# Keys and values of latents and context computed as an eighth seven-product group, with keys stored by tokens

## The chip, the cores and the metric

The kernel runs on one core of a Trainium2 chip. The metric is device time in microseconds of one execution; the kernel before takes 1354.65 us (median of three runs: 1354.47, 1354.65 and 1359.87 us). The engines are PE (TensorE matmuls), DVE (VectorE), ACT (ScalarE), POOL (GpSimd) and SP (SyncE); transfers are issued from SP, ACT and POOL, each of which has a queue of its own and works through it in program order.

## The reference, cut to what matters

One layer of a diffusion block works on 512 latent tokens `x` and 256 context tokens `ctx`, with D = 2048.

```python
shift, scale, gate = split(silu(c) @ w_ada + b_ada)          # also with c_ctx, for the context
h  = rmsnorm(x,   norm_g) * (1 + scale)   + shift            # 512 x 2048
hc = rmsnorm(ctx, norm_g) * (1 + scale_c) + shift_c          # 256 x 2048
kc, vc = hc @ w_in[:, K], hc @ w_in[:, V]                    # 4 heads of 128 each; kc is head-normed
p  = h @ w_in                                                # q, k, v, z_a, u_b, z_b, g_a, g_b
q, k = rope(rmsnorm(q)) * 128**-0.5, rope(rmsnorm(k))
attn = softmax(q @ concat(k, kc).T) @ concat(v, vc)          # 12 query heads, 4 key heads, 768 keys
y = (sigmoid(g_a) * ((attn * silu(z_a)) @ w_pa)
   + sigmoid(g_b) * ((fft2_real(u_b) * silu(z_b)) @ w_pb)) @ w_out
out = rmsnorm(x + gate * y, final_g)
```

Everything is in float32. The kernel splits each operand into a high and a low float32r part and forms a product from three matmuls (high by high, high by low, low by high).

## The kernel before, in words

**Start** (the modulation, the loop at L564). For each of the 16 blocks `kb` of 128 features, 2 MB of `w_ada` come in by two transfers (L392, from POOL for all but the first two blocks, four buffers in turn), 32 small matmuls (L476) and two turns (L486) give shift and scale, and `make_h` (L464 to L466) writes the high and low part of h for that block. Between these, `start_work` multiplies with the columns of u_b and z_b (8 tiles of 128) and of V for the latents (4 tiles): 16 blocks x 12 tiles x 3 = 576 matmuls of 128x512, whose weights come by SP (L177) and are split by ACT (L141) and DVE (L142). Partial sums are kept in SBUF by L506 and L508 after each group of blocks.

**Forms.** `form_row(j)` (L548 to L560) runs after the loop in program order, for j = 0 to 7. It adds up high and low of blocks j and j + 8 on DVE, forms S3, Z5, S2 and S4 for the seven-product scheme in one buffer `f` (one for all eight rows, L550), and stores it to `f_d` from POOL (L560). Row j + 1 writes the buffer that the store of row j reads.

**Fourier stage** (L594 to L671). `halves` (L605, L606) adds and subtracts halves of u_b, then come splits, `channels` (matmuls with `fch`), `positions` (matmuls with `fsq`), and a product with silu(z_b) (L643). Its memory lies over the buffers of the start, so its first instruction waits until those are free.

**Keys and values** (L674 to L768). Plain products: K of the latents and of the context, and V of the context, for six token tiles of K and two of V, 8 x 16 x 3 = 384 matmuls of 128x512; the context is loaded (L650 and in `context_rows`), normed and modulated here. Keys are head-normed, rotated, turned by PE (L734) and stored turned (L737).

**Seven groups by seven products** (`Group`, L821). Each takes 1024 columns of w_in (three groups of q and z_a, four of the gates g_a and g_b) and forms the 512 x 2048 by 2048 x 1024 product as two by two blocks with seven block products instead of eight. A product has four pieces of weights; a piece is 12 matmuls; a group is 7 x 4 x 12 = 336. Weights are combined in four SBUF tiles `R`, partly by transfers that add (L226, from POOL), partly by DVE (L215, L217), and split ahead of their use (L141, L142) by as many pieces as there are split buffers (3, then 5 from group 0's second product on). `job()` (L808, called at L851) runs one waiting side task after each piece.

**Attention, branches and output** (L1028 on). `get_keys` takes K and V of a group of three heads, 48 steps compute scores, softmax and values, then come the output projections, the gated merge and two more seven-product groups.

The engines run in the order that the build gives each of them; the build moves instructions ahead of others where its own model lets it. A transfer queue is served in that order too.

Of the kernel before, what the change touches and what calls it, by code (L numbers as in the profile page):

```python
# [58 lines left out]
NQZ, NGATE = 3, 4  # L59
# [7 lines left out]
def between(g, name, pc):  # L67

    f = {"P1": "Z5", "P2": "S2", "Q6": "S3", "P7": "S4"}.get(name)
    return [(f, pc - 1)] if f and g == 0 and pc in (1, 2) else []  # L70
# [4 lines left out]
def start_pieces():  # L75
# [18 lines left out]
def block_kernel(ctx, tc, xT, ctxT, x, c_row, w_ss, w_gate, vecs, qkg, rope, dft_c, dft_s,  # L94
                 w_start, w_kv, w_g, w_pab, w_o, final_g, out):
# [10 lines left out]
    bst, bpool = region("bpool", "right")  # L106
    rc = bpool.tile([P, C], F32, name="rc")
    dsc = ctx.enter_context(tc.tile_pool(name="dsc", bufs=1, space=DRAM))
    gs = dsc.tile([KK, P], F32, name="gs")
    k_d = dsc.tile([NKV, P, NKEY], F32, name="k_d")  # L110
# [26 lines left out]
    def bank2():  # L137
        return ps.tile([P, 1024], F32, tag="b2", bufs=2, name=uid("pd"))
# [58 lines left out]

    def hl_tiles():
# [4 lines left out]
        if isinstance(pool, int):  # L203
            return [Halves([pairs[2 * pool + k][i][:, :, 256:] for k in range(2)]) for i in range(2)]
# [102 lines left out]
    s_tiles = []  # L307

# [33 lines left out]
    def stream_keys(g):  # L342
        stream(("K", g), k_d[g], NKEY, 1, dst=lambda: tiles(g))
        stream(("V", g), flat(v_d[g]), NKEY, KT, dst=lambda: tiles(g))


    DONE = {"P2": (0, 0), "P7": (1, 1), "Q3": (0, 1), "Q4": (1, 0)}
    for g in range(NQZ + NGATE):
        for name in ONE_GROUP:
            if (g, name) == (NQZ + NGATE - 1, "Q4"):  # L350
                stream_keys(0)
            stream_product(name, g, w_g[g], BY_DVE_GATES)
# [28 lines left out]
    bbst, bbpool = region("bb", "right")  # L381
    bb = bbpool.tile([P, 4, T], F32, name="bb")
    pst, ppool = region("part", "right")
    part = ppool.tile([P, NS, T], F32, name="part")
    vals = ppool.tile([P, 4, T], F32, name="vals")
# [24 lines left out]
    def squares(srcs, n, r, new, run):  # L410

        acc = bank2()
        for q in range(0, KK, 2):
            a, b = new(), new()
            for t, src in zip((a, b), srcs(q)):
                nc.scalar.activation(t, src, ACT.Square)
            nc.vector.tensor_tensor(a, a, b, op=ALU.add)
            if q == 0:
                nc.vector.tensor_copy(run, a)
            else:  # L420
                nc.vector.tensor_tensor(run, run, a, op=ALU.add)
        nc.tensor.matmul(acc[:, :n], ones, run, start=True, stop=True)
        nc.scalar.activation(r, acc[:, :n], ACT.Sqrt, bias=eps_t[:, 0:1], scale=1.0 / D)
        nc.vector.reciprocal(r, r)

    def token_norms():
# [6 lines left out]
        acc = bank2()[:, :T]  # L433
# [17 lines left out]
    def spread(pick, r):  # L451
        acc = bank()
# [27 lines left out]
    def columns(acc, kb):  # L480
# [3 lines left out]
        sp = acc[:, 512:768]  # L484
# [15 lines left out]
    def start_work():  # L500
        ends = {kb + nk for kb, nk in GROUPS}
        begins = {kb for kb, nk in GROUPS}

# [6 lines left out]
        vacc = None  # L510
        for p in start_pieces():
            kb, nk, t, nt = p[2:]
            wh, wl = get(("start", p))
            if t >= 0:
                for i in range(nt):
                    acc = bank()
                    c = slice(P * i, P * i + P)
                    for k in range(nk):
                        mm3(acc, wh[:, k, c], wl[:, k, c], hhi[kb + k], hlo[kb + k], k == 0, k == nk - 1)
                    keep(pt(t + i), acc, kb == 0)  # L520
                    yield 3 * nk
            else:
                if kb in begins:
                    vacc = [bank() for _ in range(4)]
                for i in range(4):
                    c = slice(P * i, P * i + P)
                    for k in range(nk):
                        mm3(vacc[i], hhi[kb + k][:, c], hlo[kb + k][:, c], wh[:, k, :], wl[:, k, :],
                            kb in begins and k == 0, kb + nk in ends and k == nk - 1)
                    if kb + nk in ends:  # L530
                        keep(vals[:, i, :], vacc[i], kb == 0)
                    yield 3 * nk
# [9 lines left out]
    wacc = bank()  # L542
# [21 lines left out]
    for kb in range(KK):  # L564
# [22 lines left out]
    pa.close()  # L587
    for _ in work:
        pass
    for t in range(4):  # L590
        nc.gpsimd.dma_start(v_d[:, :, t, :].rearrange("g p d -> p g d"), vals[:, t, :].rearrange("p (g d) -> p g d", g=4))

    hX, lX = (lambda k: hhi[k]), (lambda k: hlo[k])

# [36 lines left out]
    def positions(g):  # L631
# [11 lines left out]
        nc.vector.scalar_tensor_tensor(alt(bb[:, g, :]), acc.rearrange("p (e s) -> p e s", e=2), 1.0 / 256.0,  # L643
                                       alt(part[:, 4 + g, :]), op0=ALU.mult, op1=ALU.mult)

    crs, crp = region("cr", "right")

    def ct_load(q):
        ct = crp.tile([P, 2, C], F32, tag="ct", bufs=2, name=uid("ct"))
        nc.sync.dma_start(ct, ctxT[:, q : q + 2, :])  # L650
        return ct[:, 0, :], ct[:, 1, :]
# [860 lines left out]
```

## Time and profile before

| | |
|---|---|
| median of three runs | 1354.65 us |
| the profiled execution | 1359.74 us, its span 1358.0 us |
| granted TensorE clock, mean | 0.994 |
| PE busy | 1319.7 us (97% of the span) |
| DVE busy | 983.8 us (72%) |
| ACT busy | 672.8 us (50%) |
| POOL busy | 145.6 us (11%) |
| moved by DMA | 294.16 MB, 217 GB/s on the mean |

A row of the timeline gives start, duration, engine, line, operation, output and input, shape and count, and in brackets the idle time before it and what ended it. A row of windows gives for each engine the busy time and the number of instructions in a stretch, then the granted clock, the share of the DMA engines' time and GB/s. Matmuls overlap in the records (a 128x512 one is recorded with about 390 ns), so their cost is read from the distance between starts.

### The profile page before, as it was taken

The numbers are of one execution on the slowest core, as the hardware profiler recorded it, in microseconds if no ns is written. First come the engines' busy times: TensorE is split into PE (matmuls) and PEld (weight loads), VectorE is DVE, ScalarE is ACT, GpSimd is POOL, SyncE is SP. The second block draws the span as 40 slices with busy tenths as digits, with TensorE's granted clock in tenths as the row PEclk, the third lists the DMA queues.
The fourth block names the chain that finished last, engine by engine and source line by source line (L and its number), as shares of the span: only waits on it lengthen the run. The fifth ranks groups of instructions, "written<-read, shape, count | busy, mean of one in ns | idle before, by whom it ended". The sixth has DMA issues, their size and how long they took to land. (4 is left out here: it accounts for less than half of the span.)

```text
span 1358.0 us, 17733 instructions
## 1 busy us (share of the span) xinstructions
PE 1319.7 (97%) x6664; PEld 1078.9 (79%) x6664; DVE 983.8 (72%) x1266; ACT 672.8 (50%) x1036; POOL 145.6 (11%) x202
## 2 busy tenths in 40 slices
PE   6999999999999999999999999999999999999996
PEld 3667688788888888888888888888888888887885
DVE  4776784868987878767566757677666689777777
ACT  5322253437555554555454545777666223364544
POOL 1011100122111020101101020000000100111210
PEclk9999999999999999999999999999999999999999
DMA  9898556857988788897879696221112889678983
GB/s 385 344 358 300 202 197 208 308 166 231 252 221 220 220 204 254 209 275 195 239 206 240 220 231 231 79 97 63 47 48 77 305 331 337 190 173 217 225 223 139
DMA packets 90085, 294.16 MB, mean 217 GB/s; under 512 B 9232, under 2 KB 22032, under 8 KB 85648
## 3 DMA queue, kind: packets, MB, share of 16 engines
q1 hardware_dynamic: 51264, 178.46, 37.9%
q0 software_dynamic: 23184, 98.59, 28.6%
q10 hardware_dynamic: 15552, 15.99, 3.5%
q8 instruction: 52, 0.85, 0.3%
q14 instruction: 33, 0.27, 0.1%
HBM read 265.73 MB, written 27.27 MB: 216 GB/s over the span
## 5 line engine op out<-in xcount | busy, mean ns | idle before, releaser
L141 ACT ACTIVATE whi<-wr 128x1024 fp32r<-128x1024 f32 (+1 forms) x151 | 158.1, 1048 | 247.2 <-PE x L272 76.9
L142 DVE TENSOR_TENSOR wlo<-wr,whi 128x1024 fp32r<-128x1024 f32 (+1 forms) x151 | 181.8, 1207 | 83.0 <-ACT whi L141 81.9
L270 PE MATMUL x<-whi,s 128*128 128x512 f32 x476 | 186.0, 391 | 0.2 <-ACT s L855 0.2
L271 PE MATMUL x<-wlo,s 128*128 128x512 f32 x476 | 185.5, 390 | 0.4 <-DVE wlo L142 0.4
L272 PE MATMUL x<-whi,s 128*128 128x512 f32 x476 | 185.3, 389 | 0.0
L270 PE MATMUL y<-whi,s 128*128 128x512 f32 x440 | 174.8, 397 | 1.3 <-ACT s L858 1.1
L271 PE MATMUL y<-wlo,s 128*128 128x512 f32 x440 | 171.8, 390 | 0.0
L272 PE MATMUL y<-whi,s 128*128 128x512 f32 x440 | 171.6, 390 | 0.0
L141 ACT ACTIVATE whi<-R 128x1024 fp32r<-128x1024 f32 x96 | 101.5, 1060 | 109.0 <-PE x L272 64.4
L142 DVE TENSOR_TENSOR wlo<-R,whi 128x1024 fp32r<-128x1024 f32 x96 | 116.8, 1222 | 39.5 <-ACT whi L141 39.4
L270 PE MATMUL x<-s,s 128*128 128x512 f32 (+1 forms) x280 | 106.5, 380 | 3.6 <-ACT s L1074 2.2
L271 PE MATMUL x<-s,s 128*128 128x512 f32 (+1 forms) x292 | 109.8, 376 | 0.0
L272 PE MATMUL x<-s,s 128*128 128x512 f32 (+1 forms) x292 | 109.1, 374 | 0.0
L271 PEld LDWEIGHTS x<-wlo,s 128*128 128x128 f32 x476 | 89.4, 188 | 19.2 <-DVE wlo L142 0.8
L270 PEld LDWEIGHTS x<-whi,s 128*128 128x128 f32 x476 | 89.4, 188 | 19.0 <-ACT s L855 0.5
L272 PEld LDWEIGHTS x<-whi,s 128*128 128x128 f32 x476 | 89.3, 188 | 18.7
L270 PEld LDWEIGHTS y<-whi,s 128*128 128x128 f32 x440 | 82.6, 188 | 21.9 <-DVE s L1110 2.7
L272 PEld LDWEIGHTS y<-whi,s 128*128 128x128 f32 x440 | 82.6, 188 | 17.5
L271 PEld LDWEIGHTS y<-wlo,s 128*128 128x128 f32 x440 | 82.7, 188 | 15.2
L226 POOL DMA_DIRECT2D R<-in_w_g x56 | 48.8, 875 | 400.2 <-DVE wlo L142 258.2
L141 ACT ACTIVATE s<-wr 128x512 fp32r<-128x512 f32 (+2 forms) x82 | 55.7, 691 | 50.5 <-PE y L272 15.4
L142 DVE TENSOR_TENSOR s<-wr,s 128x512 fp32r<-128x512 f32 (+2 forms) x82 | 61.2, 765 | 23.1 <-ACT s L141 22.1
(291 smaller groups left out, 2648.5 us busy)
## 6 DMA issues: line engine op xcount, KB each, us to landing
wr<-in_w_g SPq DMA_DIRECT2D x112, 512.0 KB, 4.5
wa<-in_w_ss POOLq DMA_DIRECT2D x28, 1024.0 KB, 9.3
R<-in_w_g POOLq DMA_DIRECT2D x56, 512.0 KB, 6.8
wr<-in_w_pab SPq DMA_DIRECT2D x32, 512.0 KB, 4.6
wr<-in_w_gate SPq DMA_DIRECT2D x32, 512.0 KB, 5.5
R<-in_w_g SPq DMA_DIRECT2D x28, 512.0 KB, 4.5
wr<-in_w_kv SPq DMA_DIRECT2D x24, 512.0 KB, 4.5
wr<-in_w_o SPq DMA_DIRECT2D x24, 512.0 KB, 7.8
```

Source lines behind the costliest of these rows:

```text
L141: nc.scalar.activation(hi, src, ACT.Copy)
L142: return nc.vector.tensor_tensor(lo, src, hi.bitcast(F32), op=ALU.subtract)
L226: nc.gpsimd.dma_start(chain[e.pc], e.nxt, accum_op=ALU.add)
L270: nc.tensor.matmul(o, ah, bh, start=start, stop=False, skip_group_check=cont)
L271: nc.tensor.matmul(o, ah, bl, start=False, stop=False, skip_group_check=cont)
L272: nc.tensor.matmul(o, al, bh, start=False, stop=stop, skip_group_check=cont)
```

## The change

- V of the latents leaves the start. `start_work` keeps only u_b and z_b (8 tiles). The four u_b tiles now stay in four PSUM banks over all 16 blocks and are copied once; the four z_b tiles go through two other banks (`bank3`).
- The whole stage of keys and values between the Fourier stage and group 0 is removed, and with it the transfers of `w_kv`.
- A group of kind "kv" is put in as number 5 of now eight (`KINDS`): K and V columns of w_in as 1024 columns, by the same seven products, with a class `Context` that adds the context's 256 rows to each product (6 more matmuls for each piece, 18 in all).
- The context is loaded twice (for its norm, then for its rows), normed, modulated and brought into eight forms in side jobs of groups 3 and 4, stored to `cf_d` from POOL and loaded again as one piece for each product of the group.
- Keys are stored by tokens. `get_keys` turns them at the attention: six turns on PE and a split, for each of the four key heads.
- `rp` and half of `fm` are opened before the last of the start's work instead of after the keys; `between` splits the forms one piece later; groups 3 to 5 have two raw weight buffers less, group 5 one more less and three split buffers instead of five.

```diff
+KINDS = ("qz", "qz", "qz", "gate", "gate", "kv", "gate", "gate")
+NQZ, KV = 3, 5
...
-        new += [(kb + i, min(2, nk), -1, 4) for i in range(0, nk, 2)]
...
-    for w, half in ((0, 0), (0, 1), (1, 1)):
-        for pc in range(8):
-            stream(("kv", w, half, pc), w_kv[w, pc], 1024, 2)
...
+        sums_u = [bank() for _ in range(4)]
...
+                whole_sum = t + i < 4
+                acc = sums_u[t + i] if whole_sum else bank3()
...
-        owed = 36 * full
-        lim = min(owed, done + 48)
+        owed = 24 * full
+        lim = min(owed, done + 32)
...
     for j in range(8):
         form_row(j)
-        for _ in range(6):
+        for _ in range(4):
             next(work, None)
     pa.close()
+    rp = ctx.enter_context(tc.tile_pool(name="rp", bufs=1, reuse_waits="tile"))
...
-    keys, kn = [], None
-    for which, half in ((0, 0), (0, 1), (1, 1)):
...
+    class Context:
...
+        def products(self, name, which, pc, w, start):
+            a = self.acc[:, 1 if which == "b" else 0, :]
+            for k in range(2):
+                j = 2 * pc + k
+                fh, fl = (f.parts[j // 4][:, j % 4 // 2, P * (j % 2) : P * (j % 2) + P] for f in self.f)
+                mm3(a, fh, fl, w[0][:, k, :], w[1][:, k, :], start and pc == 0 and k == 0, pc == 3 and k == 1,
+                    cont=not start)
...
+    def context_load(k, j, step):
+        nc.scalar.dma_start(cx["ct"][k % 2], ctxT[:, j : j + step + 1 : step, :])
...
+    def context_rows(j):
+        h, f = cx["ct"][j % 2], cx["f"]
+        for i, kb in enumerate((j, j + 8)):
+            nc.vector.scalar_tensor_tensor(h[:, i], h[:, i], gain[:, kb, 1:2], cx["rc"], op0=ALU.mult, op1=ALU.mult)
+            nc.scalar.activation(h[:, i], h[:, i], ACT.Identity, bias=shift[:, kb, 1:2])
...
+        nc.gpsimd.dma_start(cf_d[0:4, :, j, :].rearrange("f p c -> p f c"), h.rearrange("p i (s c) -> p (i s) c", s=2))
+        nc.gpsimd.dma_start(cf_d[4:8, :, j, :].rearrange("f p c -> p f c"), f)
...
     def get_keys(g):
-        kv[g] = get(("K", g)) + get(("V", g))
+        raw = get(("K", g))
+        tk = flat(pair("x"))
+        for t in range(KT):
+            nc.tensor.transpose(tk[:, t * P : (t + 1) * P], raw[:, t * P : (t + 1) * P], ident)
+        keys = tiles(g)
+        split_from(tk[:, :NKEY], *(w[:, :NKEY] for w in keys))
+        kv[g] = tuple(keys) + get(("V", g))
...
+        if g == 3:
+            context_begin()
+            context_jobs(context_squares, 1)
+            jobs.append(context_norm)
+            context_jobs(context_rows, 8)
```

More of the change, by code (lines that the diff above doesn't have):

```diff
@@ L196, in __getitem__, with int_tiles @@
             return self.parts[i[1]]
+    def int_tiles(n):
+        return [Halves([pairs[2 * n + k][i][:, :, 256:] for k in range(2)]) for i in range(2)]
     def hl_tiles():
@@ L513, in start_work @@
             wh, wl = get(("start", p))
[L514 to L532, printed above, removed]
+            for i in range(nt):
+                whole_sum = t + i < 4
+                acc = sums_u[t + i] if whole_sum else bank3()
+                c = slice(P * i, P * i + P)
+                for k in range(nk):
+                    mm3(acc, wh[:, k, c], wl[:, k, c], hhi[kb + k], hlo[kb + k],
+                        k == 0 and not (whole_sum and kb), k == nk - 1, cont=whole_sum and kb > 0)
+                if not whole_sum or kb + nk == KK:
+                    keep(pt(t + i), acc, kb == 0 or whole_sum)
+                yield 3 * nk
     def modulation(kb):
@@ L878, in run @@
                 self.done(1, 0, self.Y, self.Y)
+            if self.more:
+                self.more.end(name, which)
         def finish(self, a, form):
@@ L1064, in scores @@
         h, t = divmod(i, 4)
[L1065 removed]
+        kh, kl = kv[h // GQ][:2]
         s = slice(t * P, (t + 1) * P)
```

355 lines of the change are left out of this document (176 added, 179 removed).

## The prediction

> **What bounds the kernel now.** I read the page's first part, then the windows by stage, then the timelines of PE, POOL and DVE around the stages that the change touches.
>
> ```profile
> span 1358.0 us, 17733 instructions
> PE 1319.7 (97%) x6664; PEld 1078.9 (79%) x6664; DVE 983.8 (72%) x1266; ACT 672.8 (50%) x1036; POOL 145.6 (11%) x202
> ...
> GB/s 385 344 358 300 202 197 208 308 166 231 252 221 220 220 204 254 209 275 195 239 206 240 220 231 231 79 97 63 47 48 77 305 331 337 190 173 217 225 223 139
> ```
>
> The windows (us, then busy time and count for PE, its weight loads, DVE, ACT, POOL, then clock, DMA share, GB/s) are the start, the Fourier stage, keys and values, the second group, the fifth group:
>
> ```profile
> 24.00:200.30 176.30, 171.05 (x1086) 123.68 (x1084) 128.95 (x230) 58.01 (x85) 19.86 (x34) 0.99 0.77 288
> 200.30:222.00 21.70, 19.80 (x146) 19.18 (x147) 14.82 (x30) 10.03 (x20) 3.54 (x5) 0.92 0.49 167
> 222.00:317.90 95.90, 93.73 (x410) 75.51 (x409) 62.58 (x91) 38.63 (x54) 14.04 (x20) 0.98 0.73 241
> 470.00:546.00 76.00, 76.00 (x337) 62.91 (x336) 60.99 (x71) 40.08 (x74) 12.73 (x12) 1.00 0.82 222
> 622.00:698.40 76.40, 76.40 (x339) 63.27 (x338) 50.44 (x52) 37.98 (x45) 6.92 (x8) 1.00 0.82 224
> ```
>
> PE sets the time: a group is 336 matmuls in 76.0 us without a gap, 0.2262 us each. What PE doesn't have to issue is saved, as long as what feeds it keeps up. The borders of the stages, from PE's timeline:
>
> ```profile
> 148.99 1.93 PE L476 MATMUL pd<-wa,c 128*32 128x256 f32 x32
> 151.66 0.38 PE L486 MATMUL pd<-ident,ado 128*128 128x128 f32 x2
> ...
> 200.29 0.36 PE L270 MATMUL pb<-fch,uh 128*128 128x256 f32 x1
> ...
> 205.77 0.42 PE L270 MATMUL pb<-fsq,ah 128*128 128x256 f32 x1 [1.55 <-DVE al L142]
> ...
> 222.00 0.58 PE L270 MATMUL pd<-whi,s 128*128 128x512 f32 x1
> ...
> 317.92 0.40 PE L270 MATMUL x<-whi,s 128*128 128x512 f32 x1
> ```
>
> The start ends at 200.3, the Fourier stage at 222.0, group 0 begins at 317.9. The first two rows are block 14's matvec and turn, used below.
>
> **A chain that is hidden today.** The eight rows of forms share one buffer, so DVE writes row j + 1 only when the store of row j has landed. POOL's timeline and then DVE's:
>
> ```profile
> 121.06 0.53 POOL L392 DMA_DIRECT2D wa<-in_w_ss  x1 [8.48 <-PE pd L476]
> ...
> 124.65 0.53 POOL L392 DMA_DIRECT2D wa<-in_w_ss  x1 [0.33 <-PE pd L476]
> 125.17 0.77 POOL L560 DMA_DIRECT2D f_d<-f  x1
> ...
> 138.06 0.53 POOL L392 DMA_DIRECT2D wa<-in_w_ss  x1 [0.33 <-PE pd L476]
> ...
> 152.09 0.77 POOL L560 DMA_DIRECT2D f_d<-f  x1 [7.85 <-DVE part L508]
> 158.85 0.75 POOL L560 DMA_DIRECT2D f_d<-f  x1 [5.99 <-DVE f L559]
> ```
> ```profile
> 139.91 0.69 DVE L553 TENSOR_TENSOR f<-s,s 128x512 f32<-128x512 f32 x1 [1.86 <-DMA f_d<-f]
> ...
> 149.07 0.69 DVE L553 TENSOR_TENSOR f<-s,s 128x512 f32<-128x512 f32 x1 [1.70 <-DMA f_d<-f]
> ...
> 151.05 0.42 DVE L559 TENSOR_TENSOR f<-f,f 128x256 f32<-128x256 f32 x1
> ...
> 155.60 0.69 DVE L553 TENSOR_TENSOR f<-s,s 128x512 f32<-128x512 f32 x1 [0.45 <-DMA f_d<-f]
> ...
> 163.64 0.69 DVE L553 TENSOR_TENSOR f<-s,s 128x512 f32<-128x512 f32 x1 [2.04 <-DMA f_d<-f]
> ...
> 173.69 0.69 DVE L553 TENSOR_TENSOR f<-s,s 128x512 f32<-128x512 f32 x1 [1.97 <-DMA f_d<-f]
> ...
> 182.57 0.42 DVE L605 TENSOR_TENSOR u<-part 128x256 f32<-128x256 f32 x1 [1.92 <-DMA f_d<-f]
> ```
>
> Three things are to be seen. A store right behind weight loads on POOL's queue (four of 1 MB from 121.06 to 124.65) lands late: issued at 125.17, it releases DVE at 139.91, after 14.7 us; issued alone at 152.09, at 155.60, after 3.5. One row costs from first to first 6.5 us (149.07 to 155.60, of which 2.4 are DVE's own) to 10.1. And the Fourier stage's first instruction waits for the last store too (182.57): the whole chain stands before that stage. Today it ends 17.7 us before PE is through with the start (200.29), so nobody sees it.
>
> **The change part by part.**
>
> *Start.* 4 of 12 tiles go: 192 matmuls, 43.4 us of PE. In the built order of PE 267 matmuls instead of 387 stand before block 14's turn: 120 x 0.2262 = 27.1 us, 151.7 to 124.6 if PE alone sets the pace. The other bound is DMA: w_ada, the 8 tiles' weights and x are 46 MB, 120 us at the 385 GB/s of the fastest slice, and up to 14.7 for the last landing: 133 for block 14, 8 us later. The start's 288 GB/s is far from 385, so I take 3.5 of the 8: turn of block 14 at 128.
>
> *Forms.* What moves is POOL's order. Before, three stores stand among the weight loads; the order that the build gives the changed kernel has all eight behind the last load:
>
> ```
> before: ... wa wa f_d wa wa f_d wa wa wa wa f_d wa wa f_d f_d f_d f_d f_d
> after:  ... wa wa wa wa wa wa wa wa wa wa f_d f_d f_d f_d f_d f_d f_d f_d
> ```
>
> The last load waits for the matvec of block 13; between that and block 14's turn stand 36 matmuls (8.1 us) and a matvec (1.9), so row 0's store is issued at about 118.5, behind two loads, and lands after about 11 (nearest rows: 14.7 behind four loads, 3.5 behind none; I take a value nearer to the first): 129.5. Row 1 starts there. DVE's built order has almost nothing else between the rows: five small instructions (2.6 us) in row 1, two and a wait for ACT (1.6) in row 2, one (0.6) in row 5. Seven rows at 6.9 (2.4 of DVE, 0.5 to issue, 4.0 to land, between the 3.5 above and the 4.8 from 158.85 to 163.64) are 48.3, with those 4.8 it is 53: the Fourier stage's first instruction comes at **182**, where it comes today. Bounds: 175 (start at 125, rows of 6.5) to 193 (start at 133, rows of 7.9). The start's matmuls are done at 200.3 - 43.4 + 3.5 = 160, and what hid the chain is gone; what is late next is this stage's own preparation.
>
> *Fourier stage.* Today all of `halves` and the splits run under the start's last matmuls. DVE's built order has between the first `halves` and the first split of `channels` 8 halves (0.42 each), 4 splits of 512 and 2 of 1024, a small one, and 2 weight splits for group 0:
>
> ```profile
> L142 DVE TENSOR_TENSOR wlo<-R,whi 128x1024 fp32r<-128x1024 f32 x96 | 116.8, 1222 | 39.5 <-ACT whi L141 39.4
> L142 DVE TENSOR_TENSOR al<-pb,ah 128x512 fp32r<-128x512 f32 x8 | 5.2, 686 | 1.0 <-ACT ah L141 1.0
> ```
>
> With the first split of `al` that is 3.4 + 2.7 + 2.4 + 0.4 + 2.4 + 0.7 = 12.0 us, less 0.07 of overlap in each of 18: 10.8. `positions` then takes as long as before, 205.77 to 222.0 less the context's norm, 16.0. Group 0 begins at 182 + 10.8 + 16.0 = **209** (bounds 202 to 220) instead of 317.9: -108.9.
>
> *Keys and values.* The 95.9 us above go inside that. Group 5 adds 7 x 4 x 18 = 504 matmuls: **+114.0**. Against the 576 removed it is 72 fewer, 16.3 us. Its pieces last 4.1 us instead of 2.7, and 7 splits more of 2.3 us of ACT and DVE are hidden there, as are its evacuations.
>
> *Turns.* 24 turns leave that stage (already counted) and 24 come to the attention:
>
> ```profile
> 305.86 0.60 PE L734 MATMUL pb<-ident,kn 128*128 128x128 f32 x4
> 306.21 0.48 PE L270 MATMUL pd<-whi,hch 128*128 128x512 f32 x1
> ```
>
> Four take 0.35 us, so 2.1 in all; each of four times they also hold one of two PSUM pairs for a split. No row shows that wait: from 0 to 1 us each. I take **+3**.
>
> *Context in groups 3 and 4.* ACT's queue gets 16 loads, POOL's 16 stores; on ACT the next square or row stands behind a load's landing, and weight splits stand behind that. From below it costs nothing: splits run five pieces, 13.6 us, ahead, and ACT is busy 38 of 76 us.
>
> ```profile
> ct<-in_ctxT SPq DMA_DIRECT2D x16, 256.0 KB, 3.9
> k_d<-kt POOLq DMA_DIRECT2D x6, 256.0 KB, 3.9
> ```
>
> From above: a row needs store, load and some 3 us of work, 10.8 in three pieces of 8.2; eight times 2.6 less the 13.6 ahead is 7; and 8.4 MB more at 0.82 DMA share (224 GB/s, so 273 when full) is 31 us of transfer where two groups have 27 left: 4. I take **+3** between 0 and 11, near the end that the gapless groups show. Group 0's weights wait on SP behind loads of the forms, which wait for the last store (186): they land 15 us ahead of 209, at no cost.
>
> *Sum.* -108.9 + 114.0 + 3 + 3 = **+11** on a span of 1358.0, 1359.7 to 1371 for the profiled execution. That one lies 5 us above the median of the runs; from the median it is 1354.65 + 11 = **1366 us**.
>
> A rule of the skill speaks for less. The Trainium skill (DMA: Bandwidth & Descriptors, Anatomy of one DMA — SWDGE (gpsimd) path) gives a POOL transfer about 2.0 us plus its bytes at 436 GB/s, an estimate of 3.2 us for this 512 KB store. The rows above show 3.5 at the least and 14.7 behind loads; by the rule seven landings would be 0.8 shorter and the sum some 1360.
>
> **The rivals.**
> - *The chain is shorter and nothing else stalls.* Every store lands in the fastest row's 3.5 us, PE alone paces the start (124.6) and row 1 begins with block 14: 125 + 7 x 6.4 + 4.8 = 175, group 0 at 202, sum -115.9 + 114.0 + 2.1 = 0: **1355**. For it: DMA has little else to do after 140. Against: 4.8 from 158.85, in the same quiet. The skill's rule above points here.
> - *The chain doesn't bind* (the other side: faster). If the forms keep up with the loop, as the stores at 125 and before did, the Fourier stage follows the start's matmuls at 160, group 0 at 182: -135.9 + 114.0 + 3 + 3 = -16: **1339**. The point from which it decides: with the first `halves` later than 175 (175 + 26.8 + 114.0 + 2.1 = 317.9) the change loses even with no stall; it gains to the full only with the chain done some 15 us before the start's matmuls. Against it: all eight stores stand behind the last load, and seven rows of 6.5 don't fit between 128 and 160.
> - *The context starves the groups*: 11 instead of 3, or group 0, whose DVE work is densest, waits for its forms: **1376**.
> - *The saving isn't one*: if group 5 ran at more than 0.226 us a matmul, as with three split buffers it might, 504 at 0.25 would be 126: **1378**. Against: a piece there needs 2.3 us of splitting in 4.1.
>
> **How the numbers follow.** Forecast 0.52 (1362 to 1372); shorter chain 0.24 (1349 to 1361); no chain 0.11; starved 0.09; dear group 0.04. A measurement here can tell 0.5% (6.8 us) from no change. Slower than 1361.4 are the forecast and the last two: 0.65; within 0.5%: 0.24; faster: 0.11. The range leaves out the no-chain case and the far ends of the last two, 0.15 together, and takes in the lower bound (group 0 at 202, no stall) and the upper (220 and 3, or 209 and 11 with a dear group's 6): 1347 to 1383.
>
> **What would show it.** PE idle for about 25 us before the first `fch` matmul, from about 160; DVE's waits for the `f_d` store at seven rows and at `halves`, 20 us or more together; group 0 at 209; group 5 114 us long, groups 3 and 4 76. It is wrong if the first `halves` comes before 170, or if the groups stretch.

## The result, and the profile after

The changed kernel takes **1402.11 us** (median of four runs, 1397.06 to 1405.45) against 1355.85 us for the kernel before in its four runs: ratio 1.033, 95% interval 1.029 to 1.037. The sign was forecast, the size was not: +46 us where +11 was named, and 1402 lies above the range. The profiled execution takes 1397.06 us, 5.0 below the median of its kernel, while that of before lay 3.9 above its own; so 37 of the 46 us are to be found between the two traces.

The first part of the page after:

```profile
span 1395.3 us, 17604 instructions
PE 1313.3 (94%) x6592; PEld 1069.6 (77%) x6592; DVE 978.2 (70%) x1256; ACT 672.0 (48%) x1068; POOL 159.3 (11%) x212
...
PE   7999579999999898799998999999999999999997
...
PEclk9999789999999999899999999999999999999999
...
GB/s 387 393 378 234 166 240 225 241 204 250 198 233 198 253 275 244 219 225 162 201 178 211 266 232 233 148 65 46 77 76 1 285 337 341 223 161 215 226 233 136
```

PE works 6 us less than before and yet the span is longer: where before no digit but the first and last was under 9, the fifth and sixth slice (140 to 209 us) are at 5 and 7, the 14th (453 to 488) at 8, the 16th and 17th (523 to 593) at 8 and 7, and the 22nd (733 to 767) at 8. The clock row falls with the deepest of them, the fifth, sixth and 17th. The windows of the changed kernel, in order: the start until PE is through with it, PE's pause, the Fourier stage, the second group, then groups 3 and 4 (beside which the context is prepared), group 5 with the keys and values, and group 6:

```profile
24.00:160.30 136.30, 129.75 (x893) 86.35 (x891) 78.80 (x146) 35.01 (x52) 17.54 (x31) 0.99 0.85 325
160.30:181.10 20.80, 0.00 (x0) 0.00 (x0) 10.46 (x23) 2.87 (x5) 2.27 (x3) 0.58 0.30 100
181.10:203.20 22.10, 20.43 (x144) 19.82 (x145) 21.54 (x33) 15.42 (x24) 1.10 (x2) 0.85 0.65 220
284.30:360.40 76.10, 76.10 (x337) 63.01 (x336) 61.06 (x71) 41.00 (x76) 12.45 (x12) 1.00 0.83 223
436.50:522.80 86.30, 79.54 (x341) 64.97 (x340) 64.24 (x95) 49.31 (x80) 14.16 (x17) 0.96 0.85 245
522.80:614.30 91.50, 79.54 (x338) 64.19 (x337) 57.74 (x83) 39.18 (x52) 14.92 (x19) 0.94 0.84 235
614.30:728.50 114.20, 114.20 (x505) 94.48 (x504) 65.96 (x67) 43.12 (x68) 10.71 (x13) 1.00 0.69 183
728.50:811.90 83.40, 78.45 (x337) 63.94 (x336) 59.09 (x68) 40.86 (x71) 13.66 (x12) 0.98 0.79 229
```

The borders are read from PE's timeline by counting products: 48 matmuls take 10.88 us without a stop, seven of them 76.16. The turns are read from the start of the last group ahead of the attention to the attention's last matmul. Against the kernel before:

| step | predicted | measured |
|---|---|---|
| group 0 begins | 209 for 317.9, -108.9 | 203.2, -114.7 |
| group 5 | +114.0 | +114.2 |
| turns of the keys | +3 | +0.8 |
| groups 3 and 4 longer | +3 | +25.4 (10.1 and 15.3) |
| group 0 longer | - | +4.8 |
| group 6 longer | - | +7.2 |
| sum, on a span of 1358.0 | +11 | +37.7 (spans: +37.3) |

**The start** went as described. PE's first rows of the Fourier stage's two parts, `channels` and `positions`, then DVE's rows that lead to the first, in the changed kernel:

```profile
181.12 1.31 PE L279 MATMUL pb<-fch,uh 128*128 128x256 f32 x4 [20.83 <-ACT fch L147]
...
188.72 0.39 PE L279 MATMUL pb<-fsq,ah 128*128 128x256 f32 x1 [1.42 <-DVE al L148]
```
```profile
125.44 0.68 DVE L537 TENSOR_TENSOR f<-s,s 128x512 f32<-128x512 f32 x1
...
134.53 0.69 DVE L537 TENSOR_TENSOR f<-s,s 128x512 f32<-128x512 f32 x1 [0.78 <-DMA f_d<-f]
...
165.52 0.69 DVE L537 TENSOR_TENSOR f<-s,s 128x512 f32<-128x512 f32 x1 [3.17 <-DMA f_d<-f]
...
171.60 0.69 DVE L537 TENSOR_TENSOR f<-s,s 128x512 f32<-128x512 f32 x1 [2.95 <-DMA f_d<-f]
...
177.95 0.43 DVE L592 TENSOR_TENSOR u<-part 128x256 f32<-128x256 f32 x1 [3.94 <-DMA f_d<-f]
```

From the second row on DVE waits for the store of the row before (17.7 us together with the wait at the first `halves`, where 20 or more had been named), the first `halves` comes at 177.95, and PE, through with the start at 160.3, stands for 20.8 us. What nobody saw while the start was longer is now in the open.

**The groups** did not go as described. PE's row in group 3, and the rows of ACT that lead to it:

```profile
482.91 0.40 PE L281 MATMUL x<-s,s 128*128 128x512 f32 x1
490.06 1.22 PE L938 MATMUL y<-rope,ones 128*128 128x256 f32 x2 [6.75 <-DVE rope L934]
```
```profile
453.23 1.09 ACTq L842 DMA_DIRECT2D qz_d<-q  x2
...
457.67 0.83 ACTq L925 DMA_DIRECT2D q<-in_ctxT  x2
...
477.93 0.63 ACT L929 ACTIVATE q<-q 128x512 f32<-128x512 f32 x1 [6.16 <-DMA q<-in_ctxT]
...
487.80 0.63 ACT L929 ACTIVATE q<-q 128x512 f32<-128x512 f32 x1 [1.56 <-DMA q<-in_ctxT]
```

The context's norm is a matmul, and PE works in order: it stands before it although the weights of the next products are ready. Its squares are late: their buffer is that of the last rotated queries of group 2, whose stores are issued at 453.23, so the first load goes out only at 457.67, 21 us into the group, and the eight loads and squares then go through two buffers until 488.4. In group 4 (PE, then ACT, then DVE):

```profile
550.49 0.50 PE L280 MATMUL x<-wlo,s 128*128 128x512 f32 x1 [1.89 <-DVE wlo L148]
557.65 0.50 PE L280 MATMUL x<-wlo,s 128*128 128x512 f32 x1 [1.43 <-DVE wlo L148]
573.73 0.80 PE L279 MATMUL x<-whi,s 128*128 128x512 f32 x1 [2.41 <-ACT whi L147]
580.09 0.80 PE L280 MATMUL x<-wlo,s 128*128 128x512 f32 x1 [5.56 <-DVE wlo L148]
```
```profile
545.54 0.55 ACTq L925 DMA_DIRECT2D q<-in_ctxT  x1
546.19 0.91 ACT L947 ACTIVATE q<-q,shift 128x256 f32<-128x256 f32 x2 [10.78 <-DMA cf_d<-q]
```
```profile
578.20 0.69 DVE L800 SCALAR_TENSOR_TENSOR rope<-rope,q 128x512 f32<-128x512 f32 x1 [11.31 <-DMA rope<-in_rope]
```

ACT stands 10.78 us before it may issue a load of a context row, because the row before is still being stored from the same buffer; the weight splits behind it come late, and the third product loses 4.9 us. The table of rotations for the keys, written in the program ahead of group 5's second product, stands in the built order in the middle of group 4: its load waits for the last store of the forms, DVE waits 11.31 us for the load, and 10.4 us are lost at and in the fifth product. In group 0 it is the same instruction, for the queries:

```profile
213.84 1.29 DVE L800 SCALAR_TENSOR_TENSOR rope<-rope,q 128x512 f32<-128x512 f32 x2 [5.06 <-DMA q<-in_qkg]
```

In group 6, the waits of SP's queue and then ACT's and PE's rows:

```profile
SPq L183 <- DMA k_d<-cxe: 8.9, 1, 8.9
SPq L183 <- DMA k_d<-q: 6.1, 1, 6.1
```
```profile
760.45 1.15 ACT L147 ACTIVATE s<-wr 128x512 fp32r<-128x512 f32 x2 [8.20 <-DMA wr<-in_w_g]
```
```profile
761.14 0.79 PE L279 MATMUL x<-s,s 128*128 128x512 f32 x1 [4.50 <-ACT s L147]
```

SP stands before loads of weights into memory from which the last keys are still being stored. The kernel before has a like stop on ACT in its group 3, where PE doesn't stop; that its five full split buffers hide it is not shown by a run:

```profile
571.38 1.15 ACT L141 ACTIVATE s<-wr 128x512 fp32r<-128x512 f32 x2 [10.09 <-DMA wr<-in_w_g]
```

### The profile page after: what moved, and what is told of

Read it like the earlier page. It is cut to its first block, busy times and chain, and to the rows that moved or that the text cites. A ratio compares the mean times of both kernels' runs of the same rounds, so it can differ in the third digit from the quotient of the medians.

```text
span 1395.3 us, 17604 instructions
## 1 busy us (share of the span) xinstructions
PE 1313.3 (94%) x6592; PEld 1069.6 (77%) x6592; DVE 978.2 (70%) x1256; ACT 672.0 (48%) x1068; POOL 159.3 (11%) x212
## 4 chain that ended last, share of the span: by engine, by line
PE 80%; issue 6%; DMA 6%; DVE 3%; ACT 2%; POOL 2%; ACTq 0%; SPq 0%; POOLq 0%; DVEq 0%
PE x L279 12%; PE x L280 12%; PE x L281 12%; PE y L279 12%; PE y L280 11%; PE y L281 11%; PE tp L1126 2%; PE pd L471 2%; DMA q<-in_ctxT 1%; DMA wr<-in_w_start 1%; PE pb L280 1%; PE pb L279 1%; PE pb L281 1%; DVE wlo L148 1%; DMA wr<-in_w_g 1%
## 5 line engine op out<-in xcount | busy, mean ns | idle before, releaser
L147 ACT ACTIVATE whi<-wr 128x1024 fp32r<-128x1024 f32 (+1 forms) x129 | 135.3, 1052 | 190.4 <-PE x L281 83.8
L280 PE MATMUL x<-wlo,s 128*128 128x512 f32 x548 | 215.2, 393 | 8.9 <-DVE wlo L148 8.9
L279 PE MATMUL x<-whi,s 128*128 128x512 f32 x548 | 216.2, 395 | 3.3 <-ACT whi L147 3.1
L279 PE MATMUL y<-whi,s 128*128 128x512 f32 x544 | 215.5, 396 | 1.9 <-ACT s L742 1.1
L280 PE MATMUL y<-wlo,s 128*128 128x512 f32 x544 | 213.1, 392 | 2.9 <-DVE wlo L148 2.9
L281 PE MATMUL x<-whi,s 128*128 128x512 f32 x548 | 214.6, 392 | 0.0
L281 PE MATMUL y<-whi,s 128*128 128x512 f32 x544 | 212.7, 391 | 0.0
L148 DVE TENSOR_TENSOR wlo<-wr,whi 128x1024 fp32r<-128x1024 f32 (+1 forms) x129 | 155.9, 1212 | 68.7 <-ACT whi L147 68.4
L147 ACT ACTIVATE whi<-R 128x1024 fp32r<-128x1024 f32 x115 | 121.4, 1058 | 132.0 <-PE y L281 63.4
L148 DVE TENSOR_TENSOR wlo<-R,whi 128x1024 fp32r<-128x1024 f32 x115 | 140.0, 1220 | 55.3 <-ACT whi L147 55.1
L279 PEld LDWEIGHTS x<-whi,s 128*128 128x128 f32 x548 | 104.0, 190 | 26.0 <-ACT whi L147 3.9
L279 PEld LDWEIGHTS y<-whi,s 128*128 128x128 f32 x544 | 102.6, 189 | 26.0 <-DVE s L1150 2.1
L281 PEld LDWEIGHTS x<-whi,s 128*128 128x128 f32 x548 | 103.7, 189 | 21.8
L281 PEld LDWEIGHTS y<-whi,s 128*128 128x128 f32 x544 | 102.5, 188 | 21.6
```

Of the source, the lines that this page charges most:

```text
L147: nc.scalar.activation(hi, src, ACT.Copy)
L148: return nc.vector.tensor_tensor(lo, src, hi.bitcast(F32), op=ALU.subtract)
L279: nc.tensor.matmul(o, ah, bh, start=start, stop=False, skip_group_check=cont)
L280: nc.tensor.matmul(o, ah, bl, start=False, stop=False, skip_group_check=cont)
L281: nc.tensor.matmul(o, al, bh, start=False, stop=stop, skip_group_check=cont)
```

## Experiments

Fifteen kernels. The theory: PE loses the pause at the start to the chain of stores, and 37.4 us in the groups to separate waits, each behind a buffer that is still being stored or in an engine's order. The rivals: fewer raw weight buffers or full DMA engines starve the groups, or each stop moves on when it is removed. "Lost in 0 to 4" is the time from the start of group 0 to that of group 5 above 5 x 76.16.

| run | median us | ratio to before, 95% | group 0 begins | lost in 0 to 4 |
|---|---|---|---|---|
| changed kernel | 1402.1 | 1.033 (1.029 to 1.037) | 203.2 | 30.2 |
| e1 | 1386.5 | 1.022 (1.020 to 1.024) | 186.8 | 32.8 |
| e2 | 1377.1 | 1.015 (1.013 to 1.017) | 206.4 | 7.6 |
| e3 | 1395.3 | 1.029 (1.026 to 1.031) | 206.3 | 24.4 |
| e4 | 1393.9 | 1.027 (1.025 to 1.030) | 208.9 | 22.4 |
| e5 | 1398.2 | 1.031 (1.029 to 1.034) | 205.3 | 31.9 |
| e6 | 1399.5 | 1.031 (1.028 to 1.033) | 206.4 | 33.1 |
| e7 | 1402.9 | 1.035 (1.033 to 1.037) | 203.4 | 29.5 |
| e8 | 1354.0 | 0.9985 (0.9971 to 0.9999) | 182.3 | 11.9 |
| e9 | 1404.2 | 1.033 (1.030 to 1.036) | 205.7 | 35.2 |
| e10 | 1353.3 | 0.9977 (0.9966 to 0.9987) | 182.7 | 15.2 |
| e11 | 1351.7 | 0.9958 (0.9940 to 0.9977) | 177.7 | 16.6 |
| e12 | 1346.5 | 0.9913 (0.9897 to 0.9929) | 178.1 | 12.5 |
| e13 | 1350.2 | 0.9954 (0.9940 to 0.9967) | 181.7 | 8.2 |
| e14 | 1342.6 | 0.9902 (0.9884 to 0.9920) | 177.9 | 4.1 |
| e15 | 1346.0 | 0.9913 (0.9897 to 0.9929) | 179.8 | 8.3 |

Edits are against the changed kernel; from e8 on they add up, and line numbers lie up to eight higher. Where the start is unedited (the changed kernel, e2 to e7, e9), group 0 begins between 203.2 and 208.9 from one profile to the next, so the last column tells more about the groups than the time does. It has noise of its own: group 4, where it is unedited (the changed kernel, e1, e5, e6), loses 15.3, 17.9, 20.7 and 18.1 us, so a difference of 5 us there between two profiles shows nothing.

**e1, a second buffer for the rows of forms.**

```diff
-        f = pap.tile([P, 4, 256], F32, tag="f4", bufs=1, name=uid("f4"))
+        f = pap.tile([P, 4, 256], F32, tag="f4", bufs=2, name=uid("f4"))
```

> The only edit is a second buffer for the rows of forms. Theory (the chain of stores binds the start): PE's pause of 20.8 us ahead of the first fch matmul (160.3 to 181.1) and its stop at 155.74 go; the first halves comes within 3 us of the start's last matmul, group 0 begins at 180 to 184 instead of 203.2, and the time falls by some 20 us from 1402 to about 1381. Rival (the start's own sums or the Fourier stage's preparation bind as well): PE still pauses 10 us or more there, and under 11 us are won. The groups' own stops (38 us) stay as they are in both.

PE's row in e1:

```profile
164.63 1.02 PE L279 MATMUL pb<-fch,uh 128*128 128x256 f32 x4 [0.98 <-ACT fch L147]
```

The pause is 0.98 us for 20.83, and group 0 begins 16.4 us earlier; the time falls by 16, less than the 20 expected. DVE still stands 5.3 us before the last row, and an addition of the start behind it keeps PE until 163.6: PE's stop at 155.74, which was to go, is there with 4.0 us at 158.16. The chain is shown as the cause of the pause, the rival is out.

**e2, no preparation of the context.**

```diff
-                stream(("cf", name), cf_d[f].rearrange("p j c -> p (j c)"), 1024, 8, dst=ctx_tiles)
+                stream(("cf", name), ctxT[:, 4 * (f % 4) : 4 * (f % 4) + 4, :].rearrange("p j c -> p (j c)"), 1024, 8, dst=ctx_tiles)
...
-            context_begin()
-            context_jobs(context_squares, 1)
-            jobs.append(context_norm)
-            context_jobs(context_rows, 8)
```

> Leaves out the context's squares, norm, rows and forms in groups 3 and 4 (no loads, no cf_d stores); the seven pieces of forms that group 5 loads are raw context instead. Theory (the context's jobs stop PE): groups 3 and 4 last 76.2 us each instead of 86.3 and 91.5, group 5 stays 114.2, the time falls by 25 to about 1377. Rival (the fewer raw weight buffers of groups 3 to 5 starve PE): groups 3 and 4 stay above 80 us each, and the time stays within 10 us of 1402. The stops of group 0 (4.8) and group 6 (7.2) stay in both.

The kernel leaves the forms of the context out; group 5 multiplies raw context in their place. The time falls by 25.0, and 22.6 of the 30.2 us lost in groups 0 to 4 are gone; 5.4 of the remaining 7.6 are group 0's. The raw weight buffers are as few as in the changed kernel: that rival is out. What costs the 25 us is the side work, not the number of matmuls or buffers.

**e3, the norm five pieces later.**

```diff
+            jobs.extend([lambda: None] * 5)
             jobs.append(context_norm)
```

> Five empty jobs stand ahead of the context's norm, so that its matmul comes 5 pieces (13.6 us) later in PE's order. Theory (PE stands in its order behind a norm matmul whose squares end at 490): group 3 loses nothing, 76.2 instead of 86.3, and the time falls by about 10 to 1392, if the rows that come later cost group 4 no more than the 15.3 they cost now. Rival (the stop only moves: the squares or the rows, 13.6 us later, hold up the splits elsewhere): groups 3 and 4 together still lose 20 us or more, and the time stays at 1398 to 1406.

PE no longer stops at the norm: group 3 loses 1.6 us for 10.1, so the stop is the norm's. Group 4 loses 18.0, now in nine short stops of 0.8 to 1.8 us between 535 and 593. That lies among the 15.3 to 20.7 of the profiles in which it is unedited, so it is not shown that the rows cost more when they come later. The time falls by 6.8, less than the 10 expected, and stays under what the rival named.

**e4, the table of rotations held in group 5.**

```diff
-                rotations(qkg[:, 2:4, :], 1.0)
+                with tc.issue_after(last_split[0].ins), tc.issue_after(last_act[0].ins):
+                    rotations(qkg[:, 2:4, :], 1.0)
```

> The load and the scaling of the table of rotations for the keys, which the build had moved forward into group 4, are held behind the last weight split ahead of group 5's second product. Theory (DVE stands 11.3 us behind that load, which waits for the last cf_d store, and the splits behind it are late): the stop in group 4's fifth product (18.8 us for 10.9) goes, group 4 lasts 83 to 84, and the time falls by 8 to about 1394. Rival (the stores of the forms are late anyway, and the splits with them): group 4 stays at 90 or more, or group 5 grows by as much, and the time stays near 1402.

As the theory has it: 7.8 us less lost in the groups, 8.2 less time, and group 5 no longer than before.

**e5 and e6, the waits of group 0 and of group 6.** In e5 `rotations` only loads, and its two multiplications come at the third product, behind a split; in e6 three raw buffers join three products later.

```diff
+            elif (g, name) == (0, "P2"):
+                with tc.issue_after(last_split[0].ins):
+                    scaled()
```
```diff
-            raw_pools += [(rp, 1, "raw1", 1), (gvp, 2, "raw", 2)]
...
+            elif (g, name) == (KV + 1, "Q6"):
+                raw_pools += [(rp, 1, "raw1", 1), (gvp, 2, "raw", 2)]
```

> The two scalings of the query rotations (DVE, after a load on ACT's queue) are held behind the last weight split ahead of group 0's third product instead of standing ahead of splits for its second. Theory (in group 0 DVE stands 5.1 us behind that load, and the split behind it lets PE stop at 217.45): the second product of group 0 lasts 11 instead of 15.7 us, the time falls by about 5 to 1397. Rival (DVE is short of time in group 0 anyhow, with four forms to split there, or the weights land late): PE stops by 3 us or more elsewhere in group 0 and the time stays within 2 of 1402.

> The three raw weight buffers that group 6 takes over from the keys' rotation and from the context's sums are used from its fourth product on instead of from its start. Theory (SP's queue stands behind the stores of the last keys, 15 us, because those buffers lie over what is stored; weights for group 6's third product are late): PE's stop of 4.5 us in that product goes, group 6 lasts 76 to 77 instead of 83.4, the time falls by 6 to 7 to about 1395. Rival (the splits are short there because group 5 leaves with three split buffers instead of five, or DVE and ACT are busy with the keys): group 6 stays at 80 or more.

Both did in their place most of what was expected: the second product of group 0 takes 12.2 us for 15.7, where 11 was named, and group 6 loses 1.9 for 7.2, where under 1 was named. By the times, 3.9 and 2.6 lower, neither is told from the changed kernel: the intervals overlap.

**e7, two buffers for the derived forms of a row.**

```diff
-        h, f = cx["ct"][j % 2], cx["f"]
+        h, f = cx["ct"][j % 2], cx["f"][j % 2]
```

> The four derived forms of a context row go to two buffers in turn instead of one, and a row's load is issued three pieces behind the store that frees its buffer instead of two. Theory (DVE waits for the cf_d store of the row before, and ACT for the landing of stores ahead of its loads, and weight splits stand behind both): the stops in group 4's third and fourth product go (8.5 us), the time falls by 7 to 9 to about 1394; the stops at the norm (10) and at the table of rotations (8) stay. Rival (the accumulating weight transfers are late because the stores stand ahead of them on POOL's queue): the stops in the third product stay, and the time stays within 3 of 1402.

Nothing is gained, and the 8.5 us were misread: by products they are 7.4, of which 4.9 belong to the third product and the other 2.6 to the table of rotations (they are gone in e4). DVE's waits for the store of the derived forms are gone, and in their place it waits 3.4 us for the load of the next row, which stands behind the store of the plain forms. So there are two rings of buffers, and with the one wider the other can bind; that it does is tested in e14.

**e8, all six edits** (with three buffers for the rows of forms).

> All six edits together (rows of forms in three buffers instead of one, the norm 5 pieces later, the table of rotations held in group 5, the scaling in group 0 later, the raw buffers of group 6 later, the context's rows in two buffers with later loads). Theory (the 38 us of the groups and the 21 ahead of the Fourier stage are what is lost, each by its own cause): group 0 begins at 180 to 187, no group loses more than 2 us, the time is 1402 less 16 to 22 less 30 to 36, so 1344 to 1356, at or under the kernel before (1356). Rival (the stops move when one is mended): it stays above 1362.

1354.0 us, level with the kernel before or just under it. The causes add up: 21 us at the start and 24 in the groups are back. Group 4 still loses 9.0.

**e9 and e10, the store of the plain forms from ACT's queue**, on the changed kernel and on e8.

```diff
-        nc.gpsimd.dma_start(cf_d[0:4, :, j, :].rearrange("f p c -> p f c"), h.rearrange("p i (s c) -> p (i s) c", s=2))
+        nc.scalar.dma_start(cf_d[0:4, :, j, :].rearrange("f p c -> p f c"), h.rearrange("p i (s c) -> p (i s) c", s=2))
```

> Of each context row's two stores the one of the four plain forms is issued from ACT's queue instead of POOL's; nothing else changes. Theory (the loads of the next rows, and ACT's weight splits behind them, wait for a store that lands late because accumulating weight transfers stand ahead of it on POOL's queue, 10.8 us once): the stops in group 4's third and fourth product (8.5 us) go or fall under 3, and the time falls by 5 to 9 to about 1395. Rival (DVE's own wait for the store of the derived forms, which stays on POOL's queue, binds alone): the stops stay, and the time stays within 3 of 1402.

> The six edits of the mended kernel and the stores of the plain forms from ACT's queue. Theory (what is left in group 4, 9.0 us in its third and fourth product, is the loads' wait for stores on POOL's queue): group 4 loses under 3 us, and the time falls by 6 to 9 from 1354 to 1345 to 1348, faster than the kernel before by 0.6 to 0.8%. Rival (ACT, DVE and DMA are simply short of time with eight rows in one group): group 4 still loses 6 us or more, and the time stays above 1350.

Both miss (group 4 loses 20.6 for the 15.3 to 20.7 of the unedited kernels in e9, and 9.8 for e8's 9.0 in e10): the theory that the accumulating transfers ahead of the stores on POOL's queue make them late falls.

**e11, the Fourier stage's memory released buffer by buffer** (on e10).

```diff
-    fn, fnp = region("fn")
+    fn, fnp = region("fn", reuse_waits="tile")
```

> As the run before, and the memory of the Fourier stage waits buffer by buffer for what lay there, not for the last store of the forms as a whole. Theory (DVE stands 7.8 us at the first halves behind the last store of the forms, which makes PE stop 4.2 us at 156 because an addition of the start stands behind it): the stop at 156 falls under 1.5, group 0 begins at 175 to 179 instead of 182, and the time is another 3 to 6 lower, 1340 to 1344. Rival (one of the buffers under the first halves is that of the last row): nothing changes, within 2 of the run before.

The stop at 156 is gone, and group 0 begins at 177.7, though PE stops for 3.2 us at 158.94 in `channels`. The time falls by 1.5 only: group 4 loses 12.5 us here. ACT's row and the windows in e11:

```profile
517.42 1.06 ACT L147 ACTIVATE whi<-wr 128x1024 fp32r<-128x1024 f32 x1 [8.93 <-DMA cf_d<-q]
```
```profile
496.00:506.00 10.00, 10.00 (x46) 8.29 (x45) 8.40 (x17) 3.25 (x6) 3.53 (x5) 1.00 1.07 295
506.00:516.00 10.00, 7.76 (x35) 6.09 (x33) 2.45 (x2) 1.06 (x1) 0.67 (x1) 0.99 0.98 284
```

A weight split stands 8.9 us behind a load that waits for a store, while the DMA engines are full (1.07). Either could be the cause; four more runs were made to tell them apart.

**e12, half of the rows' stores left out, and e13, the rows spread out**, both on e11. In e12 group 5 multiplies the plain forms in place of the derived ones; in e13 the norm is 3 pieces later instead of 5 and the first four rows are 4 pieces apart.

```diff
-        nc.gpsimd.dma_start(cf_d[4:8, :, j, :].rearrange("f p c -> p f c"), f)
```

> The mended kernel with waits buffer by buffer, without the stores of the derived forms of the context (2 MB of the 8 MB that the context adds in groups 3 and 4, counting loads and stores there; group 5 multiplies the plain forms in their place). Theory (the DMA engines are full while the rows go through, and every landing is late): group 4's 9 us fall to 4 or less, the time is 1345 to 1348 instead of 1351.7. Rival (the order of waits: ACT's loads stand behind the stores of the plain forms, which stay): group 4 loses 8 to 10 us as before, the time stays at 1350 to 1353.

> All transfers stay; the norm comes 3 pieces later than in the changed kernel instead of 5, the first four rows are 4 pieces apart and the rest 3, and a row's load stands alone. Theory (DMA full in the stretch of the rows): spread over 84 instead of 65 us they leave the weights room, group 4 loses 5 us or less, the time is 1346 to 1349. Rival (each stop is a wait for one late store and doesn't care for the distance): group 4 loses 8 us or more, 1350 to 1354; or PE stops at the norm again (3 us or more in group 3).

In between in both: group 4 loses 9.1 and 6.1 for 12.5. But e8, e10 and e11, whose rows differ in the queue of one store alone, lose 9.0, 9.8 and 12.5, so e12's 9.1 shows nothing by itself. e12's time is 5.2 lower than e11's, with the intervals apart; it has fewer bytes and also one store less that a buffer waits for, and the run doesn't tell these apart. e13's time lies within e11's interval: that more room between the rows helps is not shown.

**e14, four buffers for the rows' loads** (on e11, with both stores on POOL; one raw weight buffer less in groups 3 and 4), **and e15, the same with the rows spread out.**

```diff
+        m = rp.tile([P, 1024], F32, tag="raw1", bufs=1, name="cxt")
...
-        nc.scalar.dma_start(cx["ct"][k % 2], ctxT[:, j : j + step + 1 : step, :])
+        nc.scalar.dma_start(cx["ct"][k % 4], ctxT[:, j : j + step + 1 : step, :])
```

> The mended kernel with waits buffer by buffer, both stores on POOL's queue, and four buffers for the context's loads instead of two; the two more take the place of one raw weight buffer in groups 3 and 4. Theory (ACT and the weight splits behind it wait for the landing of the store that frees a row's buffer): group 4 loses under 4 us instead of 12.5, the time is 1341 to 1345. Rival (the DMA engines are full, or the weights land late with one raw buffer less): group 4 loses 8 us or more, the time stays at 1349 to 1354.

> The same in the version with the rows spread out (norm 3 pieces later, first four rows 4 pieces apart). Theory (store ahead of load): group 4 loses under 3 us instead of 6.1, the time is 1340 to 1344. Rival (DMA full, or one raw buffer less): 6 us or more are lost there, the time stays at 1348 to 1352.

The window of e14 from group 0 to the start of group 5, and the longer of PE's two stops in it (the other is 0.93 us, in group 0); then DVE's waits in e8 just ahead of PE's two stops in group 4:

```profile
177.90:562.70 384.80, 382.44 (x1683) 315.34 (x1683) 308.36 (x387) 212.60 (x344) 63.15 (x71) 1.00 0.88 247
```
```profile
516.55 0.50 PE L281 MATMUL x<-wlo,s 128*128 128x512 f32 x1 [1.14 <-DVE wlo L148]
```
```profile
516.40 0.48 DVE L950 SCALAR_TENSOR_TENSOR q<-q,gain,rc 128x256 f32<-128x256 f32 x1 [5.49 <-DMA q<-in_ctxT]
...
535.27 0.48 DVE L950 SCALAR_TENSOR_TENSOR q<-q,gain,rc 128x256 f32<-128x256 f32 x1 [3.01 <-DMA q<-in_ctxT]
```

All of the context's bytes move, with DMA at 0.88 of its time for 0.84 in the changed kernel's groups 0 to 4, and 4.1 us are lost, 2.4 of them in group 4. With two load buffers group 4 loses 9.0 when both stores are on POOL as here (e8), and DVE waits 5.49 and 3.01 us for loads of rows; in e14's group 4 the longest such wait is 1.34 us. In both pairs, e11 and e14, e13 and e15, the time falls with four buffers, by 0.6 and 0.4% of the kernel before, and the intervals are apart. So the load's wait for its own buffer is a cause, and bytes are not needed for it; that it was the main one in group 4 rests on e14's profile. At 1342.6 us e14 is 1.0% faster than the kernel before (0.8 to 1.2%). In e15 the theory fails: group 4 loses 7.1, and DVE waits 6.6 and 3.7 us for stores of the derived forms in stretches with the DMA engines at 1.04 and 0.91. e14 has such a wait too, of 7.6 us, and loses less behind it. The profile of e14 is of an execution 1.6 us under its median, that of e15 of one 1.4 above, and by their times the two are not told apart. What decides between them in group 4 was not settled.

## Why the prediction was wrong

- **Start, right and a little better.** The end of the chain was named at 182 and came at 178. The start of the chain was 4 us early (second row at 125.4 for 129.5), the rows cost what was estimated: 52.5 us from 125.4 to 177.95 for the 53 named. The rule of the Trainium skill (DMA: Bandwidth & Descriptors, Anatomy of one DMA — SWDGE (gpsimd) path; an estimate of 3.2 us for this store) is close in the quiet part, where DVE goes on 3.4 us after the issue (174.50 to 177.95), and not with other work beside it (8.0 us, 144.71 to 152.68). From the first `halves` to the first matmul of `positions` it takes 10.8 us, as named (177.95 to 188.72), and `positions` takes 14.5 for 16.0. e1 shows that the chain was the cause.
- **Group 5, right**: 114.2, at 0.2266 us a matmul. The rival of a dear group 5 is out.
- **Turns**: 0.8 for 3. The waits for a PSUM pair, put at 0 to 1 us each, do not show.
- **Context, wrong: this step failed.** The price was +3 between 0 and 11, and it was 25.4. The bound from above counted the rows' work against splits that run 13.6 us ahead, and 4 us of bytes. Three things were missing. The norm's matmul waits in PE's own order, where no split runs ahead (10.1; e3). A load on ACT and an operation on DVE wait for a buffer that is still being stored, and everything behind them on those engines waits too, so the lead is used up not once but row after row (4.9; shown by e14 beside e8, not by e7 or e9). And the build moved the keys' table more than 50 us forward (its load stands at 571, group 5's second product begins at 631), to where only its memory, still being stored, holds it back (10.4; e4). The prediction had asked what stands behind each wait on ACT, not on PE, and had taken the place of an instruction from the program where the build had moved it.
- **Groups 0 and 6, not in the sum**: 4.8 and 7.2. The first is a two-instruction scaling 5 us too early on DVE (e5). The second is mostly SP's wait for buffers from which the last keys are being stored: used three products later, they give 5.3 of it back (e6). The kernel before has weights as late in its group 3 and loses nothing; that the three split buffers with which group 5 now ends are the difference was not tested.
- **The rival that the chain doesn't bind** had named 1339 for a kernel with group 0 at 182 and 6 us of stops and turns. That it would be so was wrong, the price was near: e14, with group 0 at 177.9 and 6.0 us lost in groups 0 to 6, takes 1342.6.
- **The chances.** The starved context was held to be worth 11 us at most, and its rival 9 in 100; the range ended at 1383 by that bound. The bound was the error, not the width. Two sums don't come out of their terms either: 8 more than the forecast is 1374 for the starved context, not 1376, and the two upper cases give 1377 and 1380, not 1383; 1402 lies above all of them.

## What to carry to other kernels

When side work is hung into a dense stream, list for each of its instructions the engine on which it stands in order, the buffer that it needs and who still reads that buffer: a wait costs what is queued behind it, and a lead of several pieces covers one such wait, not a chain of them. A matmul that depends on side work belongs some pieces after the time when that work is surely done. And read the built order for the few instructions that have no data to hold them back, such as loads of tables: a build that thinks them free puts them where they block.

## What the runs showed of the hardware

**A stop of PE can cost more than its length, and its length alone doesn't tell.** PE's rows in the changed kernel after the stop of 6.75 us (start, duration):

```profile
493.64 0.63 PE L279 MATMUL x<-whi,s 128*128 128x512 f32 x1
494.07 0.63 PE L280 MATMUL x<-wlo,s 128*128 128x512 f32 x1
494.49 0.55 PE L281 MATMUL x<-whi,s 128*128 128x512 f32 x1
494.88 0.39 PE L279 MATMUL x<-whi,s 128*128 128x512 f32 x1
495.11 0.39 PE L280 MATMUL x<-wlo,s 128*128 128x512 f32 x1
```
```profile
490.00:494.00 4.00, 3.94 (x9) 3.15 (x10) 4.00 (x7) 2.91 (x4) 0.00 (x0) 0.50 0.88 276
```

Matmuls start 0.43 us apart at a granted clock of 0.50 and, 4.8 us after the restart, 0.23 apart again: the stop of 6.75 us costs 10.1. One of 2.93 us (group 0) costs 4.8, with the slow matmuls beginning 1.2 us after the restart. Stops of 1.89 and 1.43 us (group 4) leave the clock at 1.00. Two stops of e8 and one of e10, each with the clock in a window behind it:

```profile
518.08 0.61 PE L281 MATMUL x<-wlo,s 128*128 128x512 f32 x1 [3.38 <-DVE wlo L148]
...
536.94 0.50 PE L281 MATMUL y<-wlo,s 128*128 128x512 f32 x1 [3.38 <-DVE wlo L148]
```
```profile
518.00:521.00 3.00, 2.92 (x7) 2.31 (x8) 2.83 (x8) 2.12 (x4) 0.75 (x1) 0.55 0.85 258
536.90:540.00 3.10, 3.06 (x13) 2.52 (x14) 2.70 (x7) 3.02 (x5) 2.60 (x4) 1.00 0.74 156
```
```profile
203.89 0.50 PE L281 MATMUL y<-wlo,s 128*128 128x512 f32 x1 [1.77 <-DVE wlo L148]
```
```profile
206.00:209.00 3.00, 3.00 (x10) 2.41 (x9) 2.88 (x4) 0.71 (x1) 0.00 (x0) 0.63 0.90 173
```

Of two equal stops of 3.38 us the first is followed by a clock of 0.55 and its product loses 5.3 us, the second by 1.00 and its product loses 3.7. The one of 1.77 us is followed by 0.63 and costs 3.6. The Trainium skill (TensorE: Matmul & The Clock Gate, Part 1: The HAM clock gate) gives half clock after an idle window of about 3.4 us and full clock after a busy one, the windows running freely; the two halves of the clock and the recovery agree, but the stops of 2.93 and 1.77 us show that one under 3.4 can be enough. What decides besides the length was not tested.

**A load buffer with a store behind it ties two queues together.** A store of 256 KB whose median landing is 4.9 us held its buffer for 11 (534.4 to 545.5) beside weights, and moving it to another queue gained nothing (e9, e10), while two more buffers took the loss of group 4 from 9.0 to 12.5 us (e8, e10, e11) down to 2.4 (e14).
